# Where operands begin: small tiles 128 bytes longer, a gap behind every place of weights, and four first sets put aside

## The chip, the cores and the metric

The kernel runs on one core of one Trainium2 chip. The metric is the device time of one execution in microseconds (us). An execution of the kernel before took 1042.14 us (median of three, from 1041.03 to 1042.35).

## The reference, cut to what matters

One encoder layer on 512 tokens of width 1024, all in float32: a first SwiGLU feed-forward block (FFN1, inner width 2816), a mixer block with two attentions side by side and gates, and a second SwiGLU block (FFN2). Each has its own normalisation, and scale, shift and gate vectors that are computed from a conditioning vector `c`.

```
x += 1/2 * g1 * SwiGLU_1(mod(RMSNorm(x)))
x += g2 * W_out( sig(gA) * W_A(WindowGQA+sink) + sig(gB) * W_B(DiffAttn) )
x += 1/2 * g3 * SwiGLU_2(mod(RMSNorm(x)))

def swiglu(h, w_in, w_out):
    gate, up = jnp.split(h @ w_in, 2, axis=-1)
    return (jax.nn.silu(gate) * up) @ w_out
```

## The kernel before, in words

**Three matmuls for one.** Every float32 operand of a large product is split into a rounded high part and a remainder, the low part: ScalarE casts to the high part and VectorE subtracts it (`split_from`, line 189; it is the line of nearly all CAST and subtracting TENSOR_TENSOR rows). A product is then three matmuls: high by high, low by high, high by low. In the rows of the profile `acc<-b,high` means that the streamed (moving) operand lies in a tile `b` and the weights in `high`, and that the result goes to the PSUM bank `acc`. Lines 173 to 175 are one such triple (`mm3`), lines 446 to 448 another (`two`), lines 1187 to 1189 a third.

**Stages.** FFN1 runs from the start to 345 us, with the gates of the mixers begun behind it (to 375 us). Projections, the dense differential attention and the window attention lie between 375 and 668 us, the mixers' output weights `w_mix` from 668 to 700 us, a boundary with the next normalisation to about 729 us, and FFN2 from there to 1034 us. In the feed-forward blocks the input weights are worked in units: a unit forms seven products by a Strassen-like scheme, and each product (a set, named s1, s2, s3, s4, a11, a12, a22) is 24 matmuls of 256 columns, lines 446 to 448, so that a set takes some 2.8 us. A unit's weights for s1 lie in a small tile `u4`, loaded by DMA and summed in place by a second DMA. In FFN1 three outgoing stages of 512-column matmuls (`Out1`, lines 173 to 175) stand between units; the units behind them begin at 141, 212 and 272 us.

**Where operands lie.** Weights are split into places: `parts` holds two long tiles, `high` and `low`, with five places each (`HILO`) that `high_low` hands out in turn. A place's start is 1024 elements per place, 64 more behind each of the first two places (`GAP`), plus an offset `aside` that the caller chooses: `ASIDE` is 16 elements (64 bytes), `TURN` 24 elements (96 bytes), `FAR` 64 elements. Places 2, 3 and 4 have no gap between them, so that a set which is put further aside than its neighbour reaches some elements into the neighbour's place, and the dependence tracking then makes it wait for the neighbour's readers. Streamed operands lie in tiles `b8` (12 of 8 KB a partition) and `u4` (6 of 4 KB a partition). Sums of streamed halves for a unit (`n1`, `n2` of `OPERAND`) lie in `u4` tiles too, and the sets that stream from them appear as `acc<-u,high` or `sc<-u,high`.

**Order.** The program order of TensorE is the order of the code with a planner (`line`) that puts attention steps between the projections' matmuls; ScalarE and VectorE run what a list scheduler lets through first by its own estimate. `window_turn` transposes the window attention's shares and splits them into a `u4` tile `pt`, whose halves are the streamed operand of `window_out` (rows `op<-u,b`). `branch` with `load_split` splits the weights `w_ya` while the last window blocks are still under way. Part of the gates' work at 356 to 375 us has its weights in spare `u4` tiles (`load_split` with `spare`; rows `acc<-b,u`).

Of the kernel before, what the change touches and what calls it, by code (L numbers as in the profile page):

```python
# [12 lines left out]
F32R = mybir.dt.float32r  # L13
# [5 lines left out]
P = 128  # L19
D = 1024  # L20
T = 512
NC = D // P
# [75 lines left out]
RAW, HILO, F2 = 5, 5, 8  # L98

ASIDE, TURN, GAP = 16, 24, 64  # L100
# [8 lines left out]
PLAIN, LAST_1 = 3, 4  # L109
# [24 lines left out]
def layer(ctx: ExitStack, tc: tile.TileContext, a: dict):  # L134
    nc = tc.nc
# [5 lines left out]
    def name(tag):  # L141
        count[0] += 1
        return f"{tag}_{count[0]}"

    def sbuf(tag, shape, dt, bufs):
        return sb.tile(shape, dt, name=name(tag), tag=tag, bufs=bufs)
# [7 lines left out]
    def b8(dt=F32R):  # L154
        return sbuf("b8", [P, 4, T], dt, 12)

    def u4(dt=F32R):
        return sbuf("u4", [P, 2, T], dt, 6)

    def small(n):  # L160
        return sbuf("sm", [P, 8], F32, 24)[:, 0:n]
# [4 lines left out]
    def keep(shape, nm, dt=F32):  # L166
        return sb.tile(shape, dt, name=nm, tag=nm, bufs=1)
# [20 lines left out]
    def split_from(hi, lo, src):  # L188
        last = S.copy(hi, src), V.tensor_tensor(lo, src, f(hi), ALU.subtract)  # L189
        split[:] = [i.ins for i in last]  # L190
# [5 lines left out]
    def high_low(n=1024, aside=0, holder=None):  # L196
        while turn[0] % HILO in holders:
            turn[0] += 1
        i = turn[0] % HILO
        turn[0] += 1  # L200
        if holder:
            holders[i] = holder
        i = i * 1024 + min(i, 2) * GAP + aside
        return tuple(t[:, i : i + n] for t in parts)

    def let_go(holder):
# [3 lines left out]
    def load_split(src, n=1024, spare=False, aside=0):  # L210
        raw = sbuf("raw", [P, 1024], F32, RAW)
        if spare:
            hi, lo = (u4().rearrange("p a b -> p (a b)") for _ in range(2))
        else:
            hi, lo = high_low(aside=aside)
        nc.sync.dma_start(raw[:, 0:n], src)
        split_from(hi[:, 0:n], lo[:, 0:n], raw[:, 0:n])
        return hi, lo
# [15 lines left out]
    x = [xt() for _ in range(NC)]  # L234
    parts, modv = [], []
    for nm, n in (("high", 6), ("low", 0)):
        parts.append(keep([P, HILO * 1024 + 2 * GAP + ASIDE], nm, F32R))
        modv += [keep([P, NC], f"mod{v}") for v in range(n)]

    def mod_load(v, c, w=None):  # L240
        if w is None:
            w = u4(F32).rearrange("p a b -> p (a b)")
        nc.sync.dma_start(w, a["w_mod"][v * NC + c])
        return w
# [109 lines left out]
    def new_h():  # L354
        t = [b8() for _ in range(4)]
        hh = [t[c // 4][:, c % 4, :] for c in range(NC)]
        hl = [t[2 + c // 4][:, c % 4, :] for c in range(NC)]
        return hh, hl
# [230 lines left out]
    def h_sum(t):  # L589

        p, q = SUMS[t]
        hq[t] = hq[q if t in ("t3", "t4") else p]

        h_op[t] = [u4() for _ in range(2)] if t == "n1" else b8()
        for i in range(2):
            r = slice(i * T, (i + 1) * T)
            sub(hq[t][:, r], hq[p][:, r], hq[q][:, r], t in NEGATED)
        for i in range(2):
            v = hq[t][:, i * T : (i + 1) * T].rearrange("p (k q) -> p k q", k=2)
            o = h_op[t][i] if t == "n1" else h_op[t][:, 2 * i : 2 * i + 2, :]  # L600
            split_from(o[:, :, T1], o[:, :, T2], v)
# [2 lines left out]

    cact = [sbuf("ka", [P, D], F32, 1)]
    hh, hl = new_h()
    modv += [keep([P, NC], f"mod{v}") for v in range(len(modv), 9)]
    nc.scalar.dma_start(ccol, a["c"])
    tc.keep_in_program_order(nc.scalar.dma_start(par, a["par"]))
    for c in range(NC):  # L610
# [2 lines left out]
    with tc.manual_schedule(engines=BOUND | {mybir.EngineType.SP, mybir.EngineType.Pool}):  # L613
# [12 lines left out]
        for n in range(NC):  # L626
            i, j = n // 4, n % 4
# [9 lines left out]
        def first_loads(k):  # L637
            scale = mod_load(SC1, k)
            if k == 0:
                kept.append(keep([P, NT], "pos", I32))  # L640
            shift = mod_load(SH1, k) if k == 0 else None
            raw = sbuf("raw", [P, 1024], F32, RAW)
            nc.sync.dma_start(raw, a["w1s"][k])
            w1[k] = [scale, shift or mod_load(SH1, k), raw]
# [52 lines left out]
        for k in range(3):  # L697
            first_loads(k)
# [173 lines left out]
    def in_unit1(p):  # L872
        srcs = {q: a["w1u"][p - PLAIN, i] for i, q in enumerate(("a11", "a12", "a21", "a22"))}
        u = Unit(srcs, 4, h1_operand, in_post1, p % 2)
        u.p, u.in_order = p, ('s2', 's4')
        return u

    class Out1:
# [79 lines left out]
    with tc.manual_schedule(engines={mybir.EngineType.SP, mybir.EngineType.Pool}):  # L958
# [26 lines left out]
        for n, chunks in enumerate(CHUNKS):  # L985
# [3 lines left out]
            for p in range(begun, max(chunks.stop // 2, PLAIN + 1)):  # L989
                u, nxt = units1[p], units1.get(p + 1)  # L990
# [124 lines left out]
    def gate_end(j, out):  # L1115
        t = f2()
        S.activation(t, out, AF.Tanh, scale=0.5)
        S.dma_start(gate_scr[j], t)

    gate_w = [load_split(a["w_gate"][j], spare=True) for j in range(3)]  # L1120
    gate_out = {}

# [119 lines left out]
    def turned(srcs, tag="tp"):  # L1242

        tp = bank(tag)
        for j, src in enumerate(srcs):
            PE.transpose(tp[:, j * P : (j + 1) * P], src, ident)
        line.now += len(srcs) * TR
        line.free[tag] = line.helped(0.6, 0.8)
        return tp[:, 0 : len(srcs) * P]

    def cut(src, n):
        return [src[:, j * P : (j + 1) * P] for j in range(n)]
# [109 lines left out]
    def diff_turn(h, b, p):  # L1362

        tp = turned(cut(p, NT))
        turns["b"] += 1
        g, i = h * NT // 2 + b // 2, b % 2
        if i == 0:
            pair = [u4().rearrange("p a b -> p (a b)") for _ in range(2)]
            pt_b[g] = [t.rearrange("p (k i q) -> p k i q", k=NT, i=2) for t in pair]
        hi, lo = pt_b[g]  # L1370
        with tc.high_priority():
            split_from(hi[:, :, i, :], lo[:, :, i, :], tp.rearrange("p (k q) -> p k q", k=NT))
        if i == 1:
            line.at(
                line.free["tp"] + SLACK, lambda: diff_out(h, g),
                ("op" if g % 2 == 0 else "", lambda: turns["o"] == g + h),
            )

    def diff_out(h, g):
        if g % 2 == 0:  # L1380
            out_b[h] = bank("op")
        hi, lo = pt_b[g]
        he = slice(h * P, (h + 1) * P)
        o = out_b[h][:, (g % 2) * 2 * P : (g % 2 + 1) * 2 * P]
        for k in range(NT):
            kh, kl = (t[:, k, :, :].rearrange("p i q -> p (i q)") for t in (hi, lo))
            mm3(o, vb_h[:, k, he], vb_l[:, k, he], kh, kl, k == 0, k == NT - 1)
        line.now += 2 * MM3
        turns["o"] += 1
        if g % 2:  # L1390
            t = f2()
            with tc.high_priority():
                S.copy(t, out_b[h])
            line.free["op"] = line.now + 1.0
            line.at(line.free["op"] + SLACK, lambda: diff_norm(h, t), ("op",))
# [137 lines left out]
    def span(b):  # L1533
        first, last = max(b - 1, 0), min(b + 1, NT - 1)
        return first, last - first + 1
# [59 lines left out]
    def turn_tag(b, g, kc):  # L1595
        return "acc" if (g + kc) % 2 else "tp"

    def window_turn(b, g, kc, sc):
        tag = turn_tag(b, g, kc)
        tp = turned([sc[q][:, kc * P : (kc + 1) * P] for q in (0, 2, 1, 3)], tag)  # L1600
        pt = u4()
        with tc.high_priority():
            split_from(pt[:, 0, :], pt[:, 1, :], tp)
        i = g * span(b)[1] + kc
        line.at(
            line.free[tag] + SLACK, lambda: window_out(b, g, kc, pt),
            ("op" if i == 0 else "", lambda: turns["w"] == (b, i)),
        )
        if kc + 1 == span(b)[1]:
            turns["a"] += 1  # L1610
        else:
            line.at(line.now, lambda: window_turn(b, g, kc + 1, sc), (turn_tag(b, g, kc + 1),))
# [3 lines left out]
    def window_out(b, g, kc, pt):  # L1616
        first, nk = span(b)
        if g == 0 and kc == 0:
            out_a[b] = bank("op")
        o_ps = out_a[b]  # L1620
        for kv in range(2):
            vh, vl = (v[:, first + kc, kv, :, :].rearrange("p w d -> p (w d)") for v in wa["v"])
            ph, pl = (pt[:, i, kv * 2 * P : (kv + 1) * 2 * P] for i in range(2))
            mm3(
                o_ps[:, g * 2 * P : (g + 1) * 2 * P], vh, vl, ph, pl,
                kv == 0 and kc == 0, kv == 1 and kc == nk - 1,
            )
        line.now += MM3
        if g == 1 and kc == nk - 1:
            bq = slice(b * P, (b + 1) * P)  # L1630
            oa_h, oa_l = wa["o"]
            with tc.high_priority():
                split_from(oa_h[:, :, bq], oa_l[:, :, bq], o_ps.rearrange("p (g q) -> p g q", g=4))
            line.free["op"] = line.helped(0.6, 0.8)
            done["a"] += 1
            turns["w"] = (b + 1, 0)
        else:
            turns["w"] = (b, g * nk + kc + 1)
# [244 lines left out]
    with tc.manual_schedule(engines=BOUND):  # L1883
# [6 lines left out]
        at = TO_FFN2  # L1890
# [79 lines left out]
    u = units[2]  # L1970
# [21 lines left out]
    for v, p in seq:  # L1992
# [7 lines left out]
        u = v  # L2000
# [77 lines left out]
```

## Time and profile before

| | us |
|---|---|
| median of three executions | 1042.14 |
| lowest, highest | 1041.03, 1042.35 |
| the profiled execution | 1040.55 |
| its span (first to last instruction) | 1038.8 |
| TensorE busy | 1031.9 (99%) |
| ScalarE, VectorE busy | 577.5 (56%), 786.8 (76%) |

The profiled execution lies 1.59 us below the median, and 1.75 us of it lie around the span. A row of a group gives the number of instructions, the busy time, the mean of one in ns, and the idle time ahead of it. Matmuls are pipelined, so a record of one is longer than the distance to the next one's start: rows of 276 ns stand 113.3 ns apart. Differences between two such rows are differences of that distance.

### The profile page before, as it was taken

The numbers are of one execution on the slowest core, as the hardware profiler recorded it, in microseconds if no ns is written. First come the engines' busy times: TensorE is split into PE (matmuls) and PEld (weight loads), VectorE is DVE, ScalarE is ACT, GpSimd is POOL, SyncE is SP. The second block draws the span as 40 slices with busy tenths as digits, with TensorE's granted clock in tenths as the row PEclk, the third lists the DMA queues.
The fourth block names the chain that finished last, engine by engine and source line by source line (L and its number), as shares of the span: only waits on it lengthen the run. The fifth ranks groups of instructions, "written<-read, shape, count | busy, mean of one in ns | idle before, by whom it ended". The sixth has DMA issues, their size and how long they took to land.

```text
span 1038.8 us, 18730 instructions
## 1 busy us (share of the span) xinstructions
PE 1031.9 (99%) x7342; PEld 951.0 (92%) x7342; DVE 786.8 (76%) x1436; ACT 577.5 (56%) x952; POOL 167.7 (16%) x191
## 2 busy tenths in 40 slices
PE   9999999999999999999999999999999999999998
PEld 6889899899998998899888888989999999999998
DVE  7896667567797679859772588976899777877867
ACT  6665335244455333667785855525867546655553
POOL 2101110111100100543323101001112112212210
PEclk9999999999999999999999999999999999999999
DMA  9977887967884369796637934974498998989974
GB/s 366 357 231 203 237 235 219 254 153 225 233 202 156 129 219 409 236 263 150 173 79 183 270 123 157 377 231 100 97 237 193 237 235 207 227 223 214 204 153 112
DMA packets 68793, 220.92 MB, mean 213 GB/s; under 512 B 8288, under 2 KB 10976, under 8 KB 68704
## 3 DMA queue, kind: packets, MB, share of 16 engines
q1 hardware_dynamic: 46224, 146.52, 38.5%
q0 software_dynamic: 19344, 68.70, 35.9%
q10 hardware_dynamic: 3136, 4.51, 1.2%
q8 instruction: 57, 0.93, 0.4%
q14 instruction: 32, 0.26, 0.1%
HBM read 209.46 MB, written 10.23 MB: 211 GB/s over the span
## 4 chain that ended last, share of the span: by engine, by line
PE 94%; ACT 3%; DVE 3%; issue 0%; POOL 0%; DVEq 0%; ACTq 0%; POOLq 0%
PE acc L446 7%; PE acc L447 7%; PE acc L448 7%; PE sc L447 6%; PE sc L448 6%; PE sc L446 6%; PE sc L173 5%; PE sc L174 5%; PE sc L175 5%; PE acc L173 4%; PE acc L175 4%; PE acc L174 4%; PE acc L1168 2%; PE acc L1170 2%; PE acc L1169 2%; PE acc L691 1%
## 5 line engine op out<-in xcount | busy, mean ns | idle before, releaser
L189 ACT CAST high<-raw 128x1024 fp32r<-128x1024 f32 (+2 forms) x160 | 155.9, 985 | 151.3 <-PE sc L174 44.0
L189 DVE TENSOR_TENSOR low<-raw,high 128x1024 fp32r<-128x1024 f32 (+2 forms) x160 | 181.3, 1141 | 42.0 <-ACT high L189 40.6
L446 PE MATMUL acc<-b,high 128*128 128x256 f32 x508 | 140.8, 277 | 0.0
L447 PE MATMUL acc<-b,high 128*128 128x256 f32 x508 | 140.6, 277 | 0.1
L448 PE MATMUL acc<-b,low 128*128 128x256 f32 x508 | 140.5, 277 | 0.0
L447 PE MATMUL sc<-b,high 128*128 128x256 f32 x500 | 138.2, 276 | 0.0
L446 PE MATMUL sc<-b,high 128*128 128x256 f32 x500 | 138.1, 276 | 0.0
L448 PE MATMUL sc<-b,low 128*128 128x256 f32 x500 | 138.1, 276 | 0.0
L189 ACT CAST high<-u 128x1024 fp32r<-128x1024 f32 (+1 forms) x73 | 75.4, 1036 | 50.9 <-PE sc L174 19.9
L189 DVE TENSOR_TENSOR low<-u,high 128x1024 fp32r<-128x1024 f32 (+1 forms) x73 | 87.6, 1201 | 20.8 <-ACT high L189 19.0
L173 PE MATMUL sc<-b,high 128*128 128x512 f32 (+1 forms) x272 | 97.5, 358 | 0.0
L174 PE MATMUL sc<-b,high 128*128 128x512 f32 (+1 forms) x272 | 97.2, 357 | 0.0
L175 PE MATMUL sc<-b,low 128*128 128x512 f32 (+1 forms) x272 | 97.1, 357 | 0.0
L447 PEld LDWEIGHTS acc<-b,high 128*128 128x128 f32 x508 | 95.5, 188 | 0.4 <-DVE b L1862 0.3
L446 PEld LDWEIGHTS acc<-b,high 128*128 128x128 f32 x508 | 95.4, 188 | 0.3 <-ACT f L523 0.2
L448 PEld LDWEIGHTS acc<-b,low 128*128 128x128 f32 x508 | 95.4, 188 | 0.0
L446 PEld LDWEIGHTS sc<-b,high 128*128 128x128 f32 x500 | 93.9, 188 | 0.0
L448 PEld LDWEIGHTS sc<-b,low 128*128 128x128 f32 x500 | 93.9, 188 | 0.0
L447 PEld LDWEIGHTS sc<-b,high 128*128 128x128 f32 x500 | 93.9, 188 | 0.0
L173 PE MATMUL acc<-b,high 128*128 128x512 f32 (+1 forms) x240 | 89.2, 371 | 0.2 <-DVE u L189 0.2
L175 PE MATMUL acc<-b,low 128*128 128x512 f32 (+1 forms) x240 | 86.8, 362 | 0.0
L174 PE MATMUL acc<-b,high 128*128 128x512 f32 (+1 forms) x240 | 86.6, 361 | 0.0
(398 smaller groups left out, 2714.1 us busy)
## 6 DMA issues: line engine op xcount, KB each, us to landing
u<-w_mod SPq DMA_DIRECT2D x40, 512.0 KB, 8.4
b<-w_mod SPq DMA_DIRECT2D x32, 512.0 KB, 5.5
raw<-w2i SPq DMA_DIRECT2D x31, 512.0 KB, 5.2
u<-w2i POOLq DMA_DIRECT2D x31, 512.0 KB, 6.7
raw<-w1u SPq DMA_DIRECT2D x24, 512.0 KB, 6.9
u<-w1u POOLq DMA_DIRECT2D x24, 512.0 KB, 7.3
raw<-w1o SPq DMA_DIRECT2D x24, 384.0 KB, 4.6
raw<-w_gate SPq DMA_DIRECT2D x16, 512.0 KB, 5.3
```

The source lines that it names most:

```text
L173: PE.matmul(out, wh, xh, start=first, stop=False)
L174: PE.matmul(out, wh, xl, start=False, stop=False)
L175: PE.matmul(out, wl, xh, start=False, stop=last)
L189: last = S.copy(hi, src), V.tensor_tensor(lo, src, f(hi), ALU.subtract)
L446: PE.matmul(out, wh[:, s], xh, start=first and j == 0, stop=False, skip_group_check=True)
L447: PE.matmul(out, wh[:, s], xl, start=False, stop=False, skip_group_check=True)
L448: PE.matmul(out, wl[:, s], xh, start=False, stop=last and j == 1, skip_group_check=True)
L691: PE.matmul(out1[i][:, r], w[:, i * P : (i + 1) * P], h[:, r], start=first and r.start == 0, stop=last and r.stop == T, skip_group_check=True,
L1168: PE.matmul(out[t][:, 0:n], hh[k][:, ht], wh[:, o : o + n], start=k == 0, stop=False)
L1169: PE.matmul(out[t][:, 0:n], hh[k][:, ht], wl[:, o : o + n], start=False, stop=False)
L1170: PE.matmul(out[t][:, 0:n], hl[k][:, ht], wh[:, o : o + n], start=False, stop=k == NC - 1)
```

## The change

- The tile `u4` becomes 128 bytes longer a partition, and what is put in it begins 64 bytes in (`at=ASIDE`), or at the tile's start (`at=0`) for spare weights, for pairs of the dense attention, and for the window's turned shares.
- `high_low` puts a gap behind every place. A set at `TURN` in the last place begins 32 elements earlier, so that it stays inside the tile.
- Four units of FFN1 (PLAIN, and those behind the three outgoing stages) get a set at `TURN`: s1 for the first of them, a11 for the others.
- To make room, one column vector (`mod8`) is allocated later, and the DMA scratch is halved.

```diff
-    def u4(dt=F32R):
-        return sbuf("u4", [P, 2, T], dt, 6)
+    def u4(dt=F32R, at=ASIDE):
+        return sbuf("u4", [P, 2 * T + 32], dt, 6)[:, at : at + 2 * T].rearrange("p (a b) -> p a b", a=2)
...
-        i = i * 1024 + min(i, 2) * GAP + aside
+        if aside == TURN and n == 1024 and i == HILO - 1:
+            aside = TURN - 32
+        i = i * (1024 + GAP) + aside
...
-            hi, lo = (u4().rearrange("p a b -> p (a b)") for _ in range(2))
+            hi, lo = (u4(at=0).rearrange("p a b -> p (a b)") for _ in range(2))
...
-        parts.append(keep([P, HILO * 1024 + 2 * GAP + ASIDE], nm, F32R))
+        parts.append(keep([P, HILO * 1024 + (HILO - 1) * GAP + ASIDE], nm, F32R))
...
-    modv += [keep([P, NC], f"mod{v}") for v in range(len(modv), 9)]
+    modv += [keep([P, NC], f"mod{v}") for v in range(len(modv), 8)]
...
             if k == 0:
+                modv.append(keep([P, NC], "mod8"))
...
         u.p, u.in_order = p, ('s2', 's4')
+        u.turned = {PLAIN: ("s1",), PLAIN + 2: ("a11",), PLAIN + 4: ("a11",), PLAIN + 6: ("a11",)}.get(p, ())
...
-            pair = [u4().rearrange("p a b -> p (a b)") for _ in range(2)]
+            pair = [u4(at=0).rearrange("p a b -> p (a b)") for _ in range(2)]
...
-        pt = u4()
+        pt = u4(at=0)
...
-    nc = bacc.Bacc("TRN2", target_bir_lowering=False, num_devices=1, dynamic_dma_scratch_size=4096)
+    nc = bacc.Bacc("TRN2", target_bir_lowering=False, num_devices=1, dynamic_dma_scratch_size=2048)
```

In addresses (bytes, modulo 128): `b8`, the dense part of `high` and `low`, and the other streamed tiles begin at 64 before and after; sets at `ASIDE` have their weights at 0, at `FAR` at 64, at `TURN` at 32. The `u4` tiles begin at 32 before, and what lies in them begins at 64, or at 0 for `at=0`, now. So by (streamed, weights): the `<-u,high` sets of both feed-forward blocks go from (32, 0) to (64, 0); the gates with weights in `u4` from (64, 32) to (64, 0); `window_out` from (32, 64) to (0, 64); the set at 743 us with weights in a `b` tile from (32, 64) to (64, 64); the four turned sets of FFN1 to (64, 32), the first of them from (32, 0), the others from (64, 0).

The instructions stay the same, and their order is the same on TensorE, GpSimd and SyncE. On ScalarE and VectorE some splits of weights move, as the place that they write is free earlier. On ScalarE, at 631 to 637 us, where the last window blocks run beside the first product with `w_ya` (`raw_845` is a quarter of these weights, `u4_795`, `u4_797`, `u4_799`, `u4_813` and `u4_818` are turned shares of the window attention in the banks `acc` and `tp`), there stands before:

```order
L189 CAST u4_795_6479<-acc_794_6474 128x512
L189 CAST u4_797_6493<-tp_796_6488 128x512
L189 CAST u4_799_6507<-acc_798_6502 128x512
L189 CAST u4_813_6558<-tp_812_6553 128x512
L189 CAST high_86<-raw_845_6800 128x1024
L189 CAST u4_818_6578<-acc_817_6573 128x512
```

The same place on ScalarE after the change:

```order
L189 CAST u4_795_6479<-acc_794_6474 128x512
L189 CAST u4_797_6493<-tp_796_6488 128x512
L189 CAST high_86<-raw_845_6800 128x1024
L189 CAST u4_799_6507<-acc_798_6502 128x512
L189 CAST u4_813_6558<-tp_812_6553 128x512
L189 CAST u4_818_6578<-acc_817_6573 128x512
```

The cast of the weights has moved ahead of two casts of turned shares. On VectorE at the same place (the ISA rows reduce the window's scores, `sm_810` and `sm_811` lead to the exponentials of the next block) there stands before:

```order
L1674 SCALAR_TENSOR_TENSOR b8_725_6099<-f2_792_6465,acc_793_6467 128x512
L189 TENSOR_TENSOR u4_799_6507<-acc_798_6502,u4_799_6507 128x512
L1559 ISA x_805_6527,sm_800_6510<-sc_801_6511,u4_647_5713 128x256
...
L1559 ISA x_808_6533,sm_800_6510<-acc_804_6514,u4_647_5713 128x256
...
L189 TENSOR_TENSOR u4_813_6558<-tp_812_6553,u4_813_6558 128x512
L1570 TENSOR_TENSOR sm_811_6537<-sink_3223,sm_810_6536 128x4
L1571 TENSOR_SCALAR sm_810_6536<-sm_810_6536 128x4
L189 TENSOR_TENSOR low_93<-raw_845_6800,high_86 128x1024
L189 TENSOR_TENSOR u4_818_6578<-acc_817_6573,u4_818_6578 128x512
```

And after the change:

```order
L1678 SCALAR_TENSOR_TENSOR b8_725_6099<-f2_792_6465,acc_793_6467 128x512
L189 TENSOR_TENSOR low_93<-raw_845_6800,high_86 128x1024
L189 TENSOR_TENSOR u4_799_6507<-acc_798_6502,u4_799_6507 128x512
L1563 ISA x_805_6527,sm_800_6510<-sc_801_6511,u4_647_5713 128x256
...
L189 TENSOR_TENSOR u4_813_6558<-tp_812_6553,u4_813_6558 128x512
L1563 ISA x_808_6533,sm_800_6510<-acc_804_6514,u4_647_5713 128x256
...
L189 TENSOR_TENSOR u4_818_6578<-acc_817_6573,u4_818_6578 128x512
L1572 TENSOR_TENSOR sm_810_6536<-sm_800_6510,rqa_76 128x4
```

The subtraction for these weights now stands ahead of that for `u4_799` and of the four score reductions. Two similar moves, at 60 to 80 us (a set's high part two casts earlier, another's low part nine rows later) and at 436 us (two splits of projection weights in another order), are of the same kind.

## The prediction

> **What bounds the kernel now.** I read the page's busy times first, then the waits of TensorE.
>
> ```profile
> PE 1031.9 (99%) x7342; PEld 951.0 (92%) x7342; DVE 786.8 (76%) x1436; ACT 577.5 (56%) x952; POOL 167.7 (16%) x191
> PE acc L620 <- POOL ident masks.py:199: 1.4, 1, 1.4
> 746.00:1034.00 288.00, 288.00 (x2533) 1.00 0.87 203
> ```
>
> TensorE is busy for 99% of the span, and its longest wait, at the start, is 1.4 us; what else the view of waits lists is shorter than 0.4 us each. The last row, a window over FFN2, has no gap at all: 2533 matmuls in 288.00 us, 113.7 ns each, at a granted clock of 1.00. So there is no wait to win; time comes from how far one matmul stands behind another, or from a new wait.
>
> That distance is not one number. In the timeline of TensorE these rows each begin a set of 24 matmuls of 256 columns, and the next row of the fence (or the one named) begins the next set:
>
> ```profile
> 141.06 0.39 PE L175 MATMUL sc<-b,low 128*128 128x512 f32 x1
> 141.29 0.28 PE L446 MATMUL acc<-b,high 128*128 128x256 f32 x1
> 144.12 0.28 PE L446 MATMUL sc<-u,high 128*128 128x256 f32 x1
> 146.92 0.28 PE L446 MATMUL acc<-b,high 128*128 128x256 f32 x1
> 149.65 0.28 PE L446 MATMUL acc<-b,high 128*128 128x256 f32 x1
> 152.37 0.28 PE L446 MATMUL sc<-b,high 128*128 128x256 f32 x1
> 163.25 0.28 PE L446 MATMUL acc<-u,high 128*128 128x256 f32 x1
> 729.20 0.28 PE L446 MATMUL acc<-b,b 128*128 128x256 f32 x1
> 732.08 0.28 PE L446 MATMUL sc<-b,high 128*128 128x256 f32 x1
> 743.16 0.28 PE L446 MATMUL tp<-u,b 128*128 128x256 f32 x1
> 746.03 0.28 PE L446 MATMUL acc<-b,high 128*128 128x256 f32 x1
> ```
>
> I name a set by where its streamed operand and its weights begin, in bytes modulo 128. The set (64, 0) right behind the 512-column stage takes 2.83 us, 118 ns a matmul (141.29 to 144.12). The set (32, 0) that streams from a `u` tile takes 2.80, 117 ns. From 149.65 to 163.25 five sets of the same kind (64, 0) take 13.60, 113.3 ns each. So (64, 0) has two paces, a tight one of 113.3 and a wide one of about 117.7, and in this trace either lasts until something disturbs it. The set at 729.20, (64, 64), takes 2.88 (120 ns), that at 743.16, (32, 64), 2.87 (119.6).
>
> What changes the pace is seen in the rows of the groups, cut to windows (a record of 276 ns is the tight pace, one of 281 the wide one):
>
> ```profile
> L173 PE MATMUL acc<-b,high 128*128 128x256 f32 x31 | 8.6, 276 | 0.0
> 662.37 0.33 PE L173 MATMUL acc<-b,high 128*128 128x256 f32 x1
> 662.53 0.28 PE L174 MATMUL acc<-b,high 128*128 128x256 f32 x1
> L173 PE MATMUL acc<-b,high 128*128 128x256 f32 x15 | 4.2, 281 | 0.0
> ```
>
> The first row is from 651.7 to 662 us, the last from 663 to 668, of one and the same product. Between them stands one distance of 160 ns. A single short hold turned the tight pace into the wide one, to the end of the stage. By contrast each set that streams from 32 brings the tight pace: 117 ns before 146.92, 113.3 soon after it. I find that behind all two dozen of them, and the wide pace behind each step from 512 columns straight to (64, 0) (141, 212, 272 and 700 us).
>
> **The change part by part, against the profiled execution (1040.55 us, its span 1038.8).** It lies 1.59 below the median, so the sum is carried to the median at the end.
>
> *FFN2's sets from `u`, now (64, 0).* All groups of these sets have nearly the same mean:
>
> ```profile
> L446 PE MATMUL acc<-u,high 128*128 128x256 f32 x48 | 13.4, 279 | 0.0
> L448 PE MATMUL sc<-u,low 128*128 128x256 f32 x40 | 11.2, 280 | 0.0
> 757.02 0.28 PE L446 MATMUL sc<-b,high 128*128 128x256 f32 x1
> 757.38 0.28 PE L446 MATMUL sc<-b,high 128*128 128x256 f32 x1
> ```
>
> The first two rows are from 746 us on: three rows of 48 and three of 40, 264 matmuls. In the tight pace each gains 279.5 - 276 = 3.5 ns, 0.9 us. The last two rows show the settling behind such a set: three matmuls in 0.36 us, not 0.34; 16 places, some of them shorter, make about 0.2. Together -1.1.
>
> *FFN1's sets from `u`.* Seven sets of 24. Four stand within tight stretches: 4 x 24 x 3.5 ns is 0.34, with settling -0.4. The other three are the second sets behind the outgoing stages, and there they are what ends the wide pace (144.12 above). With (64, 0) the wide pace goes on, 118 ns, through this set and the next two, until a11, which begins at 152.37 and now is (64, 32). The two sets from 146.92 to 152.37 lose 48 x 4.4 ns = 0.21, a11 itself some 24 x 4 ns = 0.10. Times three: +0.9. That a11 ends the wide pace rests on these rows, from 715.9 to 723 us, where (64, 32) is followed by (64, 0):
>
> ```profile
> 722.29 0.28 PE L448 MATMUL acc<-b,low 128*128 128x256 f32 x1
> 722.41 0.28 PE L446 MATMUL sc<-b,high 128*128 128x256 f32 x1
> ...
> 722.76 0.28 PE L446 MATMUL sc<-b,high 128*128 128x256 f32 x1
> 722.88 0.28 PE L447 MATMUL sc<-b,high 128*128 128x256 f32 x1
> 722.99 0.28 PE L448 MATMUL sc<-b,low 128*128 128x256 f32 x1
> ```
>
> Up to 722.41 the (64, 32) rows stand 120 apart, as flat as a (64, 64) set; three matmuls later, from 722.76, the distance is 113 (722.76 to 722.99 is 0.23 for two). Five of seven such entries in the trace go tight, two wide. The first unit's s1, (32, 0) to (64, 32), is 117 ns before and after: 0.
>
> *The set at 743.16, now (64, 64):* 2.87 against 2.88 us of the set at 729.20: 0. What matters is the pace that it leaves behind. The rows above say tight: a distance of 120 up to 722.41, and the tight pace from there. I take tight, and come back to it under the rivals.
>
> *Gates with weights in `u`, and `window_out`.*
>
> ```profile
> L174 PE MATMUL acc<-b,u 128*128 128x256 f32 x48 | 13.5, 281 | 0.0
> L174 PE MATMUL op<-u,b 128*128 128x256 f32 x72 | 20.2, 281 | 0.0
> L1188 PE MATMUL acc<-low,b 128*128 128x256 f32 x96 | 26.9, 280 | 0.0
> L1189 PE MATMUL acc<-high,b 128*128 128x256 f32 x96 | 26.8, 279 | 0.0
> ```
>
> The 144 matmuls of the gates, (64, 32), now are (64, 0): at 276 they gain 5 x 144 = 0.7 us, at 281 nothing. These stages are cut by small transposes, behind which either pace occurs, so -0.4. The 216 of `window_out` become (0, 64). The last two rows are (0, 64) today, 279.5 against 281 and more for `op<-u,b`: 216 x 1.5 to 2 ns = -0.4. Bounds: 0, and 216 x 5 ns = -1.1 if they reached 276.
>
> *The moves on ScalarE and VectorE.* At 631 us the cast of `raw_845` now stands ahead of that of `u4_799`, so whoever waits for the latter waits for the DMA of the former.
>
> ```profile
> 629.26 0.33 SPq L216 DMA_DIRECT2D raw<-w_ya  x1
> raw<-w_ya SPq DMA_DIRECT2D x1, 512.0 KB, 3.5
> 633.32 0.69 DVE L189 TENSOR_TENSOR u<-acc,u 128x512 fp32r<-128x512 f32 x1
> 635.44 1.05 ACT L189 CAST high<-raw 128x1024 fp32r<-128x1024 f32 x1
> 636.66 1.23 DVE L189 TENSOR_TENSOR low<-raw,high 128x1024 fp32r<-128x1024 f32 x1
> 635.40 0.60 PE L1246 MATMUL acc<-ident,x 128*128 128x128 f32 x4
> ```
>
> Issued at 629.26 with 3.5 us to landing, the weights are there at 632.8. The cast (1.05) ends at 633.8, the subtraction (1.23) at about 635.1, that for `u4_799` (0.69) at 635.7 instead of 634.0. TensorE's transposes at 635.40 reuse the bank that this one frees, so they are 0.3 late. The score reductions and the next block's exponentials follow some 2 us later than before; one more bank is freed at 637.7, needed at 637.6. I take +0.4. Bounds: 0 if the DMA lands 0.5 us earlier; +1.8 if it takes 4.9, the median of all eight `w_ya` transfers on the page's list. The other two moves I cost at nothing. At 60 to 80 us VectorE does the same work in another order, and the next step behind it is this subtraction, whose first user on TensorE is the second row:
>
> ```profile
> 78.77 1.21 DVE L189 TENSOR_TENSOR low<-raw,high 128x1024 fp32r<-128x1024 f32 x1
> 84.26 0.28 PE L448 MATMUL sc<-b,low 128*128 128x256 f32 x1
> ```
>
> It is done at 80.0 and wanted at 84.3, a cover of 4.3 us, three such subtractions. At 436 us ScalarE is idle ahead of the two splits that change places, and both end no later than before.
>
> *DMA scratch and `mod8`.* No transfer is on TensorE's waits; 0. If half the scratch held GpSimd's transfers back, their cover is that the code asks for a unit's s1 nine sets ahead, 9 x 2.8 = 25 us; a delay beyond that would be a wait, and is part of the first rival.
>
> Sum: -1.1 - 0.4 + 0.9 - 0.4 - 0.4 + 0.4 = -1.0. The profiled execution would be 1039.55; the median 1042.14 - 1.0 = 1041.1.
>
> **The rivals.**
>
> *FFN2 locks in the wide pace (slower).* Today every few sets a (32, 0) set sets the pace right; in the new kernel no set between 746 and 1034 us does. If the set at 743.16 leaves the wide pace, or any short hold like the one at 662.37 comes later, everything behind it stands 117.7 apart. From 746 on: 2533 - 264 matmuls x 4.4 ns = +10.0 in place of the gain of 1.1, so 1041.1 + 1.1 + 10.0 = 1052.2; from half way, about 1046.5. It decides when one wait of TensorE comes in FFN2. For it: 512-column (64, 64) rows are followed by the wide pace each time, and a (64, 64) set of 256 directly ahead of (64, 0) does not occur in this trace. Against it: the rows at 722, the same distance of 120 and the tight pace; and no hold in FFN2 today. 0.18, two thirds of it from the start.
>
> *a11 does not end the wide pace in FFN1 (slower).* Then the wide pace goes on to the next outgoing stage or the end of FFN1: at nine, nine and thirteen sets of 24, 744 matmuls x 4.4 ns = +3.3: 1044.4. Two of seven entries speak for it; 0.07.
>
> *More is won.* `window_out` at 276, all gates tight, no wait at 635: -0.7 - 0.3 - 0.4 on top, 1039.7, and down to 1039.0 if part of the wide stretches vanishes as well. 0.12.
>
> *Where operands begin changes nothing.* If the streams of operands and the loads of weights did not disturb each other wherever they begin, every set would take the same time, and only the wait at 635 would be left: 1042.14 + 0.4 = 1042.5. This is what the Trainium skill says ("SBUF — State Buffer", section "Who interferes with whom"): two independent read ports for streamed operand and weights, and a TensorE that waits on no one. The trace does not agree: 120 ns from 729.20 and 113.3 from 149.65, for the same shape. 0.03.
>
> A page on the size of the gain: the Trainium skill ("TensorE: Matmul & The Clock Gate", section "Back-to-back issue gap") gives N / 2.4 + 2.5 ns for one matmul alone, which is 109.2 for 256 columns. The tight pace here is 113.3; were that reached, an estimate by that page is 264 x 7.8 ns = 2.1 us in FFN2 instead of 0.9; no row of this trace shows it.
>
> **How the numbers follow.** The forecast as summed has 0.60, its own range 1039.6 to 1043.3 (the wait at 635 from 0 to 1.8, the gates and the window from nothing to all, the executions' own scatter of 0.6). The whole range, 1039.0 to 1046.5, takes in a11's failure and a lock from half way; left out are a lock from the start (0.12) and small tails. A measurement of this kernel can tell about 0.2% from no change, that is 1040.06 and 1044.22. Faster: 0.20 of the forecast (a small wait, gates mostly tight) and the 0.12: 0.32. Slower: 0.18 + 0.07 = 0.25. Within: 0.40 + 0.03 = 0.43.
>
> **What would show it.** In the new profile: records of `<-u,high` at 276 in FFN2 and the window from 746 on with 2533 matmuls in about 286.9 us (a lock: 298); 281 from each outgoing stage to a11 and 276 behind it; `op<-u,b` at 279 to 280; a wait of some 0.3 us of TensorE on VectorE at about 635. The prediction is wrong if the rows behind 746 are 281, if a11's followers are 281, or if TensorE's waits in all grow by more than 2 us.

## The result, and the profile after

The changed kernel takes 1051.55 us (median of 4, 1049.07 to 1052.1), the kernel before 1041.74 in the same measurements: a ratio of 1.0087, interval 1.0074 to 1.0099. The forecast of 1041.1 and its range up to 1046.5 were missed; the first rival, FFN2 in the wide pace from its beginning (1052.2), is what happened.

The page of the changed kernel and its view of waits. The profiled execution is the one of 1049.07 us, with a span of 1047.3:

```profile
PE 1040.2 (99%) x7342; PEld 958.8 (92%) x7342; DVE 786.8 (75%) x1436; ACT 577.5 (55%) x952; POOL 167.5 (16%) x191
PE acc L622 <- POOL ident masks.py:199: 1.4, 1, 1.4
PE acc L173 <- DVE u L189: 0.3, 1, 0.3
PE acc L694 <- ACT b L681: 0.3, 1, 0.3
```

No new wait: TensorE is busy 8.3 us longer (1031.9 before), with the same 7342 matmuls in the same order. So the start of any matmul can be compared with the start of the same one before. Lines 446 to 448 are now 448 to 450. In the timeline of TensorE:

```profile
744.21 0.28 PE L448 MATMUL tp<-u,b 128*128 128x256 f32 x1
747.08 0.28 PE L448 MATMUL acc<-b,high 128*128 128x256 f32 x1
964.49 0.28 PE L449 MATMUL tp<-b,high 128*128 128x256 f32 x1
964.61 0.28 PE L450 MATMUL tp<-b,low 128*128 128x256 f32 x1
964.90 0.39 PE L448 MATMUL sc<-b,high 128*128 128x256 f32 x1
965.12 0.28 PE L449 MATMUL sc<-b,high 128*128 128x256 f32 x1
```

The set at 743.16 of the prediction, here called the lead's s1 (the unit that is `lead` in the code), begins at 744.21: 1.05 us were lost by then. The set behind it begins at 747.08 (746.03 before). And this is how FFN2 went on, in a window from there to 964.5 us and in one behind the two unusual distances at 964.61 (0.29 us) and 964.90 (0.22). The row of a group below each window is from 748 to 964 us and from 966 to 1042:

```profile
747.08:964.50 217.42, 217.42 (x1849) 217.42 (x1848) 169.85 (x250) 127.03 (x190) 39.94 (x46) 1.00 0.90 214
L448 PE MATMUL acc<-b,high 128*128 128x256 f32 x238 | 66.9, 281 | 0.0
965.20:1042.00 76.80, 76.80 (x679) 76.80 (x678) 62.01 (x103) 41.26 (x66) 11.26 (x13) 1.00 0.70 150
L448 PE MATMUL acc<-b,high 128*128 128x256 f32 x76 | 21.0, 276 | 0.0
```

217.42 us for 1849 matmuls is 117.6 ns each: the wide pace, records of 281, for 218 us without a break. Then one short hold of TensorE turned it into the tight one, and the rest ran at 76.80 / 679 = 113.1 ns, records of 276. The 679 matmuls at 4.5 ns less are 3.0 us, less 0.3 for the hold. This fits the 2.4 to 3.0 us by which this execution lies below the other three (1051.44 to 1052.1); that these ran wide to the end is not shown, as only this one has a profile.

In FFN1 the groups read as follows, in five windows: right behind the first outgoing stage (141.4 to 144 us), ahead of its a11 (147.3 to 152.3), behind that a11 (155.5 to 163), behind the a11 of the second stage (226.8 to 234), and further on in the second stage, behind the next set from `u` (239 to 249):

```profile
L448 PE MATMUL acc<-b,high 128*128 128x256 f32 x8 | 2.2, 281 | 0.0
L450 PE MATMUL acc<-b,low 128*128 128x256 f32 x15 | 4.2, 281 | 0.0
L448 PE MATMUL acc<-b,high 128*128 128x256 f32 x8 | 2.2, 276 | 0.0
L448 PE MATMUL acc<-b,high 128*128 128x256 f32 x8 | 2.2, 281 | 0.0
L448 PE MATMUL acc<-b,high 128*128 128x256 f32 x8 | 2.2, 276 | 0.0
```

In the second window the kernel before was tight already. a11 ended the wide pace behind the first stage (276), and behind the third it did too. Behind the second the pace stayed wide (281) for three more sets and the set from `u`, and only behind that set was it tight (276). A set from `u` in the tight stretch, finally, in two halves (163.45 to 164.6 us and 164.9 to 166):

```profile
L448 PE MATMUL acc<-u,high 128*128 128x256 f32 x4 | 1.1, 276 | 0.0
L449 PE MATMUL acc<-u,high 128*128 128x256 f32 x4 | 1.1, 280 | 0.0
```

The first half streams from one small tile and runs tight, the second from the next tile and runs nearly as wide as the wide pace. A tile of 4224 bytes is not a multiple of 256: the streams of every other tile begin at 64 modulo 256, those between at 192. The prediction had looked at addresses modulo 128 only.

### The profile page after: what moved, and what is told of

Read it like the earlier page. It is cut to its first block, busy times and chain, and to the rows that moved or that the text cites. A ratio compares the mean times of both kernels' runs of the same rounds, so it can differ in the third digit from the quotient of the medians.

```text
span 1047.3 us, 18728 instructions
## 1 busy us (share of the span) xinstructions
PE 1040.2 (99%) x7342; PEld 958.8 (92%) x7342; DVE 786.8 (75%) x1436; ACT 577.5 (55%) x952; POOL 167.5 (16%) x191
## 4 chain that ended last, share of the span: by engine, by line
PE 92%; ACT 4%; DVE 4%; issue 0%; POOL 0%; DVEq 0%; ACTq 0%; POOLq 0%
PE acc L448 7%; PE acc L449 7%; PE acc L450 7%; PE sc L448 6%; PE sc L450 6%; PE sc L449 6%; PE sc L173 5%; PE sc L174 5%; PE sc L175 5%; PE acc L173 4%; PE acc L175 4%; PE acc L174 4%; PE acc L1174 2%; PE acc L1173 2%; PE acc L1172 2%; PE acc L694 2%
## 5 line engine op out<-in xcount | busy, mean ns | idle before, releaser
L448 PE MATMUL acc<-b,high 128*128 128x256 f32 x508 | 142.3, 280 | 0.0
L449 PE MATMUL acc<-b,high 128*128 128x256 f32 x508 | 142.2, 280 | 0.1
```

Source lines behind the costliest of these rows:

```text
L448: PE.matmul(out, wh[:, s], xh, start=first and j == 0, stop=False, skip_group_check=True)
L449: PE.matmul(out, wh[:, s], xl, start=False, stop=False, skip_group_check=True)
```

## The experiments

From here on (a, b) modulo 256 are the beginnings of stream and weights in bytes; the dense weights are at 128. Times are medians; "before" is the kernel before in the same measurements.

**e1: FFN2's sums n1 back at 32 modulo 128**

```diff
-        h_op[t] = [u4() for _ in range(2)] if t == "n1" else b8()
+        h_op[t] = [u4(at=at) for _ in range(2)] if t == "n1" else b8()     # at=8 in FFN2
```

> The changed kernel, but in FFN2 the sums n1 (streamed by the lead's s1 and by every later set s1) begin again 32 bytes past a multiple of 128. Theory (the lead's s1 leaves the wide pace at 746 us and no later set ends it): the sets from 32 end it, FFN2 goes back to 113.3 ns, records of 276 from 746 us on, time about 1042.8 us (1041.7 and the 1.05 us that the changed kernel has lost by 746). Rival (the gaps behind the places, the order on ScalarE and VectorE or the halved DMA scratch slow FFN2): stays near 1051.

1048.84 us (before 1041.27, ratio 1.0074, 1.0059 to 1.0090). Neither of the two numbers expected. The groups, from 762 to 775 us and from 781.5 to 795, between sets from `u`:

```profile
L448 PE MATMUL acc<-b,high 128*128 128x256 f32 x21 | 5.9, 281 | 0.0
L448 PE MATMUL sc<-b,high 128*128 128x256 f32 x31 | 8.6, 276 | 0.0
```

The lead's s1, from 32, leaves the tight pace again; but the next set from `u` turns tight into wide, the one behind it wide into tight, and so on in turn. In the kernel before, both tiles of n1 are at 160, and each set leaves the tight pace. Here they are at 160 and 32. So the theory's first half (the lead) stands, its second (a set from 32 ends the wide pace) holds only for tiles that agree modulo 256.

**e2: all small tiles at 64 modulo 256 (tiles 256 bytes longer, gaps of before)**

```diff
-        return sbuf("u4", [P, 2 * T + 32], dt, 6)[:, at : at + 2 * T]...
+        return sbuf("u4", [P, 2 * T + 64], dt, 6)[:, at : at + 2 * T]...   # at=48
-        i = i * (1024 + GAP) + aside
+        i = i * 1024 + min(i, 2) * GAP + aside
```

Without the gaps a turned set reaches eight elements into the next place, so some weights of that place are overwritten; only the time is read.

> The changed kernel, but each small tile grows by 256 bytes instead of 128 and its operands begin so that all six tiles have their streams at 64 modulo 256 (in the changed kernel every other tile is at 192); to make room, the gaps are those of before. No set streams from 32. Theory: in FFN2's lead s1 the second tile, at 192, is what leaves the wide pace; with both at 64 the set is flat at 120 ns to its end and the pace behind it is tight, as at 722 us; all later sets from u run at 113.3: FFN2 from 746 us takes some 286.9 us, in all about 1041.5 us. Rival (without any set from 32 FFN2 runs wide wherever the small tiles begin): 1051 to 1052. Rival (gaps and order): also near 1042, but then e1 stays at 1051.

1051.81 us (ratio 1.0102, 1.0087 to 1.0117): the first rival's number. The window over FFN2 that took 288.00 us in the kernel before:

```profile
747.44:1045.54 298.10, 298.10 (x2533) 1.00 0.85 197
```

Its lead runs flat, that is each matmul 120 ns behind the last, to the end, as was expected, and yet the pace behind it is wide, and stays so for all of FFN2. That the lead's second tile was the cause fell with this: a lead at (64, 64) modulo 128, flat or not, leaves the wide pace.

**e3: gaps and scratch alone, every operand where it was**

```diff
-        i = i * 1024 + min(i, 2) * GAP + aside
+        i = i * (1024 + GAP) + aside
-    ... dynamic_dma_scratch_size=4096)
+    ... dynamic_dma_scratch_size=2048)
```

> The kernel before with only the gap behind every place and the halved DMA scratch: every operand begins as before modulo 256, and ScalarE and VectorE have the changed order. Theory: nothing to be seen, 1041.7 within 0.6, no new wait at 635 us. Rival (gaps, order, scratch): the loss shows here, up to 1050.

1041.51 us (10 executions, ratio 1.0003, 0.9994 to 1.0012), FFN2 at 276 and the waits those of before:

```profile
PE 1032.7 (99%) x7342; PEld 952.0 (92%) x7342; DVE 786.8 (76%) x1436; ACT 577.7 (56%) x952; POOL 167.3 (16%) x191
L448 PE MATMUL acc<-b,high 128*128 128x256 f32 x316 | 87.2, 276 | 0.0
```

Gaps, halved scratch and the moves on ScalarE and VectorE cost nothing that can be seen.

**e4: one set more turned, a12 of FFN2's unit 2**

```diff
+    units[2].turned = ("a12",)
```

> The changed kernel with one set more turned: a12 of FFN2's unit 2, the second set behind the lead's s1, has its weights 32 bytes past a multiple of 128. Theory: it ends the wide pace in most executions (in the changed kernel's profile two of three turned sets in FFN1 did): then 1043 to 1044, otherwise 1051; runs may differ by 8 us. Rival (the streams from u bring the wide pace back each time): 1051 in every run.

1042.21 us, nine of ten executions between 1041.05 and 1043.02, one at 1050.54. That is less than the 1043 to 1044 expected. FFN2's groups, from 754.2 to 756.6 us, from 760 to 780, and in the last two rows from 748 to 1030:

```profile
L448 PE MATMUL sc<-b,high 128*128 128x256 f32 x8 | 2.2, 281 | 0.0
L448 PE MATMUL acc<-b,high 128*128 128x256 f32 x28 | 7.7, 276 | 0.0
L448 PE MATMUL sc<-b,high 128*128 128x256 f32 x288 | 79.5, 276 | 0.0
L449 PE MATMUL acc<-u,high 128*128 128x256 f32 x48 | 13.3, 278 | 0.0
```

One set of 24 matmuls with its weights 32 bytes aside takes back 9.3 of the 9.8 us that the change had lost. This is the decisive run: the same streams, gaps, order and lead, and the tight pace from 760 us to the end. But the turned set did not bring it at once. It ends at 754.05 us, and the set behind it is still wide (281); the set from `u` behind that one begins wide as well, and only after it, from 759.71 us on, is the pace tight, as in FFN1's second stage. In the changed kernel the same set from `u`, without a turned set ahead, left the wide pace as it was. So the turned set is what made the difference, but what it changed does not show in the records of 281 right behind it. The 278 of the sets from `u` is half 276 and half some 280, the second tile.

**e6: only the growth of the tiles, operands at 32 modulo 128 as before**

```diff
+        return sbuf("u4", [P, 2 * T + 32], dt, 6)[:, 0 : 2 * T].rearrange("p (a b) -> p a b", a=2)
```

> The kernel before with only the growth of the small tiles by 128 bytes (and the halved scratch for room): operands in them stay at 32 modulo 128, but every other tile is 128 bytes further modulo 256. Theory (the growth alone breaks what righted the pace, as the profile of e1 shows: such a set changes tight into wide and wide into tight): 1049 to 1051, with the stretches between sets from u in FFN2 at 113.3 and 117.8 in turn. Rival (only the move from 32 to 64 matters): 1041.5.

1048.84 us (before 1041.21, ratio 1.0077, 1.0062 to 1.0091), with 281 and 276 in turn in the windows from 762 and from 781.5 us:

```profile
L446 PE MATMUL acc<-b,high 128*128 128x256 f32 x22 | 6.2, 281 | 0.0
L446 PE MATMUL sc<-b,high 128*128 128x256 f32 x32 | 8.8, 276 | 0.0
```

The growth by 128 bytes alone, with every operand at the same place modulo 128, loses 7.6 us, a little less than was expected.

**e9: only the move of the streams, tiles of the old size, all at 64 modulo 256, no newly turned set**

```diff
+    keep([P, 40], "pad0")        # ahead of the small tiles, on top of e3
...
+                keep([P, 24], "pad1")        # 64 elements with pad0: 256 bytes
```

> The kernel e5_one_class without any newly turned set: all streams from small tiles at 64 modulo 256 and tiles of the old size, so that the move from 32 to 64 stands alone. Theory (the sets from 32 are what ends the wide pace): FFN2 wide from 746 us to the end, +10.0; FFN1 wide from each step out of 512 columns to the next, some 820 matmuls and 7 sets from u, +4.3: about 1055 to 1056, slower than the changed kernel. Rival (streams at 64 in all tiles keep the tight pace by themselves, only the tiles at 192 spoil it): 1040.

1056.67 us (before 1041.76, ratio 1.0146, 1.0132 to 1.0160), within a microsecond of what was expected. FFN2's groups are at 281 from 748 to 1030 us, those of FFN1 from 160 to 163 us too:

```profile
L448 PE MATMUL acc<-b,high 128*128 128x256 f32 x292 | 82.1, 281 | 0.0
L449 PE MATMUL tp<-b,high 128*128 128x256 f32 x8 | 2.3, 281 | 0.0
```

So growth and move each are enough to lose FFN2, in two ways: the growth makes sets from `u` turn the pace over, the move takes from them that they set it right.

**e7: e4 without the turned sets of FFN1**

```diff
-        u.turned = {PLAIN: ("s1",), PLAIN + 2: ("a11",), PLAIN + 4: ("a11",), PLAIN + 6: ("a11",)}.get(p, ())
```

> The changed kernel with the one turned set in FFN2 (e4), but without the turned sets of FFN1. Theory: each wide pace in FFN1 then lasts from 512 columns to the next 512 columns, some 820 matmuls x 4.4 ns more than with them: 1045.8, that is 3.6 us above e4. Rival (the turned a11 does little): within 1 us of e4's 1042.2.

1045.10 us (1044.46 to 1046.35), 2.9 us above e4, where 3.6 were expected. By the starts of the same matmuls in the two traces, some 1.5 us are lost in the first unit, whose turned set is s1, and some 2.5 behind the three outgoing stages, where it is a11. The four turned sets of the change do what they are there for, if not each time at once.

**e5, e8, e10: all streams at (64, 128), and turned sets where the pace is to be set**

```diff
+    keep([P, 40], "pad0")        # with pad1 as in e9, on top of e3
...
+        u.turned = {PLAIN: ("s1",), PLAIN + 1: ("s2",), PLAIN + 3: ("s2",), PLAIN + 5: ("s2",)}.get(p, ())
...
+    units[2].turned = ("a12",)
```

> The kernel before with gaps and halved scratch, the small tiles at their old size but all moved so that their streams begin at 64 modulo 256, and turned sets (weights at 32 modulo 128) only where the pace has to be set: the first set of each FFN1 unit behind 512-column matmuls (s1 of the first, s2 behind the three outgoing stages) and a12 of FFN2's unit 2. Theory (what keeps the tight pace is that streams at 64 and weights at 128 modulo 256 follow one another, and a turned set right behind 512 columns ends the wide pace each time): FFN2 -1.1 us against before but for the lead and two sets behind it, +0.2; FFN1's seven sets -0.7; in all 1039.7, 0.9985 of before, in nearly every run. Rival (a long stretch without sets from 32 does not keep the tight pace): 1045 or more.

1040.08 us (before 1041.21): eleven of twelve executions from 1038.64 to 1041.12, one at 1049.30, so that the ratio (0.9996, 0.9981 to 1.0010) tells no gain; 1039.7 was expected. Groups from 752 to 800 us and, in the second row, the sets from `u` from 748 to 1030:

```profile
L449 PE MATMUL sc<-b,high 128*128 128x256 f32 x63 | 17.4, 276 | 0.0
L448 PE MATMUL acc<-u,high 128*128 128x256 f32 x48 | 13.2, 276 | 0.0
```

Here the turned a12 brought the tight pace at once, in FFN2 from 751.4 us on. With both tiles at 64 the sets from `u` run at 276 all through, and the tight pace held for 280 us with no other set to right it. The rival of this run, that it would not hold, is refuted for eleven executions of twelve.

```diff
+    units[2].turned = ("a12", "s2")
```

> e5_one_class with one set more turned in FFN2, s2 of unit 2, six sets behind the turned a12. In 11 of 12 executions e5 took 1038.6 to 1041.1 us, in one 1049.3. Theory (that one execution is a wide pace that the single turned set did not end): a second turned set ends it, all executions lie within 1039 to 1041.5, the median within 0.2 us of 1040.1, as a turned set entered in the tight pace costs 24 x 6.7 ns = 0.16 us at most. Rival (something else, at any place, makes an execution long): one in ten stays near 1049.

1040.12 us, ten of eleven executions from 1038.97 to 1040.70, one at 1050.90. A second turned set soon behind the first did not remove the odd execution; that the first set fails now and then is not its explanation, or not the whole of it.

```diff
+    for u in (units[2], units[4], units[6], units[9]):
+        u.turned = ("a12",)
```

> e5_one_class with the turned a12 in units 2, 4, 6 and 9 of FFN2, at about 749, 801, 877 and 973 us. Of e5 and e8 one execution in eleven or twelve took 9 to 11 us more, with a profile for none of these. Theory (in that execution FFN2 ran wide from its beginning on, though a turned set stood there): a wide pace now ends at 801 at the latest, after 52 us x 3.9% = 2.0 us, and a later one lasts at most 96 us, 3.7 us; three more turned sets cost 3 x 0.17 us; so median 1040.6 and no execution above 1045. Rival (the 9 to 11 us come from elsewhere): an execution near 1050 shows up again, if there are as many executions.

1040.61 us, eleven executions from 1039.70 to 1041.50 (before 1041.79): ratio 0.9988, 0.9979 to 0.9997. The median is the expected one, a tenth of a per cent below the kernel before, with an interval that just leaves out 1. No execution near 1050 came up; but with three such in 33 executions of e4, e5 and e8, eleven without one would come up by chance about one time in three. What makes them stays open: none of the three has a profile.

## Why the prediction was wrong

*The step that failed* is "the rows above say tight" for the set at 743.16. It took the rows at 722 us as the precedent for what a flat set leaves behind. Those were flat, but with their weights at 32 modulo 128; the lead's are at 64. The distance of 120 is the same, what follows is not: behind (64, 64) of 256 columns the wide pace came in every profile that has it (the changed kernel, e2, e4, e5, e7, e8, e9, e10), and behind a lead from 32 the tight one in every other (before, e1, e3, e6). The rows that did speak of (64, 64), the 512-column ones with the wide pace behind them each time, stood in the prediction as the argument for the rival, and were the nearer precedent. Which of the differences made the rows at 722 go tight was not varied alone.

*The rival* was sized rightly: +10.0 and 1052.2 forecast, 1051.55 measured, and 281 in 1849 matmuls on end. For FFN2 by itself e2, wide to the end, shows 298.10 us where the prediction had named 298. Its condition was right too: no set ends the wide pace any more, though a hold at 964.61 us did. That a turned set would have led out of it is e4. What was wrong is its chance, 0.18. That the total came within 0.7 us is in part luck: FFN1 lost 0.9 more than forecast and gates and window won 0.4 less, while the 0.4 for the moves did not come, and the kernel before took 1041.74 here, not 1042.14.

*FFN2's sets from `u`, -1.1.* Not seen, as they ran wide with all others. Where the tight pace held (e4) they are at 278, half the gain: the term overlooked that the grown tiles alternate modulo 256, and that (192, 128) runs at 280. With the tiles alike (e5) they are at 276, the full term.

*FFN1, -0.4 + 0.9.* Forecast +0.5 by the end of FFN1; the same matmul begins 1.4 us later there (at 346.8 us before). Behind the first stage the loss by the end of a11 is 0.31 as worked out (0.21 + 0.10). The difference comes from the second stage, which a11 left wide as far as the next set from `u` (+0.3 more), from the sets from `u` that gained 0.03 each instead of 0.09, and from a hold near 314 us, which stands in both traces but turned tight into wide only in the new one (+0.3). The rival that a11 never helps was put at +3.3; its removal in e7 costs some 2.5 behind the three stages, against e4, where a11 failed to act at once in one of them.

*Gates -0.4, `window_out` -0.4.* Measured by the shift of the same matmuls: -0.1 across the gates, -0.3 from 492 to 668 us. In e3, where no operand begins elsewhere, the gates shift by -0.2 as well and the stretch from 492 to 668 us not at all. So of the gates' term nothing is shown, and that of `window_out` was right in sign and sized a little too large.

*The moves on ScalarE and VectorE, +0.4.* The mechanism is there, its price is not. Rows of the changed kernel:

```profile
630.30 0.33 SPq L218 DMA_DIRECT2D raw<-w_ya  x1
633.03 1.05 ACT L189 CAST high<-raw 128x1024 fp32r<-128x1024 f32 x1 [0.47 <-PE acc L174]
635.40 0.69 DVE L189 TENSOR_TENSOR u<-acc,u 128x512 fp32r<-128x512 f32 x1
636.45 0.60 PE L1250 MATMUL acc<-ident,x 128*128 128x128 f32 x4
```

The cast waited for TensorE (0.47) and not for the DMA, which had landed within 2.7 us of its issue, not 3.5. The subtraction for `u4_799` ended at 636.1, and TensorE wanted it at 636.45. The prediction had that subtraction end at 635.7, which is 636.7 on the clock of this trace, 1.04 us behind: the estimate from the group's landing time put it 0.6 us too late, and the whole term was smaller than that. The same matmul is 1.04 us behind at 630 us and 1.03 at 640.

*"Where operands begin changes nothing"* (0.03) is refuted by e9 and e6: beside gaps and scratch, which cost nothing in e3, only beginnings differ there, for 14.9 and 7.6 us. The Trainium skill ("SBUF — State Buffer", section "Who interferes with whom") has TensorE's two read ports independent; these runs show that the distance of two matmuls depends on where the stream begins (e9) and on where the weights begin (e4). That the two reads disturb each other would explain it, and is not shown by itself.

## What to carry to other kernels

Where TensorE is busy throughout and a matmul of one shape stands at two distances in the trace, look first for what switches between them, and only then at which set is slower: the sets that looked 3 ns too slow were the ones that put all others right, and taking their cost of 1.1 us away lost some ten. A precedent in a trace counts when both operands begin where they do in the case, not when the distance agrees. And before a long stretch is left without anything that resets its state, a cheap reset (here 24 matmuls with weights 32 bytes aside, at most 0.17 us: 120.1 ns a matmul against 113.3 in e10, entered from the tight pace) is worth its price, even one that acts in some nine of ten executions only.

## What the runs showed of the hardware

- Matmuls of 256 columns with streams and weights at (64, 128) modulo 256 run at 113.3 ns or at 117.8, and keep either for hundreds of microseconds (218 us wide in the changed kernel, 280 us tight in e5). The half of a set that streams from 192 has records of 278 to 280 in a tight stretch too (164.9 to 166 us of the changed kernel).
- A single hold of TensorE can turn the pace either way: at 964.61 us wide became tight (0.29 and 0.22 us), at 662.37 us in the kernel before tight became wide (0.16). It need not: at 939.48 us in e4 (0.34 and 0.22 us) tight stayed tight.
- Sets from two tiles at 160 set the tight pace whatever the pace was (in the kernel before, behind the wide set at 141.29 us and throughout FFN2); sets from tiles at 160 and 32 turn the one into the other (e1, e6).
- A turned set entered from the wide pace, with all streams at 64, left the tight one at once in the profiles of e5, e8 and e10. With tiles at 64 and 192 in turn it did so behind two of FFN1's three stages in the changed kernel; where it did not (the second stage there, FFN2 in e4 and e7), the next set from `u` left the tight pace, 117.9 ns a matmul itself and 113.6 in the set behind it. Without a turned set ahead, such sets from `u` left the wide pace wide (the changed kernel from 754 to 964 us). By their times, nine of e4's ten executions came out of the wide pace.
